# A planner that orders all instructions of a hybrid LRU, GLA and SSD backbone, with new prices for its instructions

## The chip, the core and the metric

The kernel runs on one core of one Trainium2 chip. A core has TensorE (PE in the profile, with its weight loads as PEld), VectorE (DVE), ScalarE (ACT), GpSimd (POOL) and a queue on SyncE (SP) that issues the DMAs. The engines run side by side, each through its own instructions in the order of the program, and wait for each other by semaphores. The metric is the device time of one execution in microseconds; the tables give the median of the runs.

## The reference

Two layers (`DEPTH` 2) over 512 latent tokens and 256 context tokens of width 1024. Each layer normalises and modulates the tokens, projects them once to 13408 columns, mixes them in three branches (an RG-LRU, a chunked gated linear attention GLA, and a Mamba-2 SSD, each in both directions), gates and projects each branch, merges them and projects the sum. Layer 1 returns only the latent tokens, so it needs the context only as far as its states go.

```python
for l in range(DEPTH):
    need_ctx = l < DEPTH - 1
    shift, scale, gate = jnp.split(jax.nn.silu(c) @ ada_w[l] + ada_b[l], 3, axis=-1)
    h_lat = _rmsnorm(x_lat, pre_g[l]) * (1.0 + scale[:, None]) + shift[:, None]
    h_ctx = _rmsnorm(x_ctx, pre_g[l]) * (1.0 + scale_c) + shift_c
    s_l = _split_cols(h_lat @ p['w_in'])          # and s_c of h_ctx
    # three branches, context first, their states handed to the latent scans
    y = LRU(s[0]), GLA(s[2], s[3], s[4], s[6]), SSD(s[8], s[9])
    pa = (ya * jax.nn.silu(s[1])) @ p['w_pa']
    pb = (_rmsnorm(yb, gla_norm_g) * jax.nn.silu(s[5])) @ p['w_pb']
    pc = _rmsnorm(yc * jax.nn.silu(s[7]), ssd_norm_g) @ p['w_pc']
    g = jax.nn.sigmoid(s[10])
    o = (g[0] * pa + g[1] * pb + g[2] * pc) @ p['w_out']
    x_lat = x_lat + gate[:, None] * _rmsnorm(o_lat, post_g[l])
```

## The kernel before

**The work.** All of it is float32. A large product is made of three passes of float32r matmuls: both operands are split into a high part (a cast) and a low part (the difference), and high x high, low x high and high x low are summed in PSUM. Weights come in items of 128 x 1024 numbers (512 KB): a DMA from SP loads one into one of two `raw` buffers; `splitter` cuts it into two halves and splits each into `wh` (a cast, by ACT or DVE, `copy`, L328 or L329) and `wl` (a subtraction on DVE, `sub`, L343), four buffers of each; `main` issues the matmuls of the items (`mm`, L388). One item of layer 0 is 24 pairs of matmuls with 256 and 512 columns; one of layer 1 that needs only the latent tokens is 24 with 512 columns. Results stand in two PSUM tiles `pp`, which an engine must empty before the next item but one can begin.

**The branches.** The SSD branch works in four groups: states (`ssd_update`: POOL makes `xw`, a copy and a subtraction split it into `xwh` and `xwl`, PE multiplies), masks (`ssd_ms`: a DMA broadcasts rows `cumd` into `rr`, ACT adds biases in eight steps of 128, DVE selects, ACT takes the exponential, POOL multiplies), outputs (`ssd_scan`: `y`, `yi`) and a group norm. GLA and LRU follow. In the LRU and merge part, `it_out` multiplies by `w_pa`; its tail needs a gate tile that an SP load brings back from DRAM (`load_gate`), and `gate_rows` sends a gain row to DRAM and back (`gpd`, `gp`). Then come the output projection and the residual (`it_wout`, `post`).

**What sets the order.** No order is written by hand. Every piece of work is a generator (a stream) that offers one instruction after another with a price in ns, and `loop` plans the whole program before it runs: it holds a modelled time for each engine and each tile, and of all instructions on offer it puts next the one that can start first by the model. `start_of` gives that start: the engine's free time, or the end of what writes or reads the tiles on another engine plus `LAT` (200 ns) and a slack by engine (1200 ns for PE, 100 for DVE and ACT, 0 for POOL and SP). Where an instruction can go to two engines (`any_op`: ACT or DVE for a copy, DVE or POOL for some subtractions), the one with the earlier modelled end gets it. Ties go to the stream with the higher rank. Each engine then runs its instructions in the order planned; the prices reach the chip in no other way.

```python
            for c in ins:
                if c.we != eng and c.w + slack > r:
                    r = c.w + slack
...
                    for w, (eng, cost, _) in enumerate(c[1]):
                        t = self.start_of(eng, c[2], c[3], LAT + SLACK[eng])
                        if w == 0 or t + cost < t0 + c0:
                            t0, c0, w0 = t, cost, w
                    k = (t0, 0 if s.urgent and s.urgent() else s.prio, s.seq)
                    if best is None or k < best[0]:
                        best = (k, s, w0)
```

The prices stand with the helpers: `any_op` (L206 to L211) for DMAs, whose modelled queue moves 360 bytes a ns and whose landing is put 2000 ns after that; `act` (L315), `copy` (L328) and `affine` (L335) for ACT; `sub` (L345), `tt` and `ts` for POOL; `vcost` for DVE; `mm` (L386) for PE.

Of the kernel before, what the change touches and what calls it, by code (L numbers as in the profile page):

```python
# [9 lines left out]
F32R = mybir.dt.float32r  # L10
I32 = mybir.dt.int32
AF = mybir.ActivationFunctionType
ALU = mybir.AluOpType
AX = mybir.AxisListType
PSUM = bass.MemoryType.PSUM
# [125 lines left out]
class Sched:  # L141
# [48 lines left out]
    def any_op(self, ways, outs, ins):  # L190

        outs = [self.cell(o) for o in outs]
        ins = [self.cell(i) for i in ins if i is not None and not isinstance(i, (int, float))]
        yield ("op", ways, outs, ins)
        eng, cost, emit = ways[self.way]
        start = self.start_of(eng, outs, ins)
        if eng == "PE":
            if start - self.eng_free[eng] > HAM_WINDOW:
                self.warm_up = HAM_WINDOW
            if self.warm_up > 0:  # L200
                cost *= 2
                self.warm_up -= cost
        extra = emit()
        if isinstance(extra, int):
            cost += extra
        if eng == "SP":  # L206
            self.eng_free[eng] = start + 470
            self.dma_free = max(start, self.dma_free) + cost
            fin = self.dma_free + 2000
        else:  # L210
            fin = self.eng_free[eng] = start + cost  # L211
        self.now = max(self.now, start)
        for c in outs:
            if fin > c.w:
                c.w, c.we = fin, eng
        for c in ins:
            if fin > c.r:
                c.r, c.re = fin, eng
# [56 lines left out]
class Mixer(Sched):  # L275
# [30 lines left out]
    def act(self, out, in_, func, bias=None, scale=None, accum=None):  # L306
        kw = {}
        if bias is not None:
            kw["bias"] = bias
        if scale is not None:  # L310
            kw["scale"] = scale
        if accum is not None:
            kw["accum_out"] = accum
        aps = sum(not isinstance(x, (int, float)) for x in (bias, scale) if x is not None)
        cost = 0.83 * out.free_size() + 60 + 90 * aps  # L315

        def emit():
            st = ACT_SETS.get(func)
            self.nc.scalar.activation(out, in_, func, **kw)  # L319
            if st and st != self.act_set:  # L320
                self.act_set = st
                return ACT_LOAD
        yield from self.op("ACT", [out] + ([accum] if accum is not None else []), [in_, bias, scale], cost, emit)

    def copy(self, out, in_):

        n = out.free_size()
        yield from self.any_op([("ACT", 0.83 * n + 60, lambda: self.nc.scalar.copy(out, in_)),  # L328
                                ("DVE", self.vcost(n, in_, True), lambda: self.nc.vector.tensor_copy(out, in_))],  # L329
                               [out], [in_])  # L330

    def affine(self, out, in_, scale, bias):

        n = out.free_size()
        yield from self.any_op([("ACT", 0.83 * n + 240, lambda: self.nc.scalar.activation(  # L335
                                    out, in_, AF.Identity, scale=scale, bias=bias)),
                                ("DVE", self.vcost(n, in_, True) + 120, lambda: self.nc.vector.tensor_scalar(
                                    out, in_, scale, bias, ALU.mult, ALU.add))], [out], [in_, scale, bias])

    def sub(self, out, a, b, pool=False):  # L340

        n = out.free_size()
        ways = [("DVE", self.vcost(n, a), lambda: self.nc.vector.tensor_tensor(out, a, b, ALU.subtract))]  # L343
        if pool:
            ways.append(("POOL", 2.3 * n + 50, lambda: self.nc.gpsimd.tensor_tensor(out, a, b, ALU.subtract)))  # L345
        yield from self.any_op(ways, [out], [a, b])

    def vcost(self, n, x, fast=False):
        return (0.52 if fast and x.space != PSUM else 1.04) * n + 69

    def tt(self, out, a, b, op, pool=False):
        eng = self.nc.gpsimd if pool else self.nc.vector
        cost = 2.3 * out.free_size() + 50 if pool else self.vcost(out.free_size(), a)
        yield from self.op("POOL" if pool else "DVE", [out], [a, b], cost, lambda: eng.tensor_tensor(out, a, b, op))  # L354

    def stt(self, out, a, s, b, op0, op1):
# [2 lines left out]

    def ts(self, out, a, s1, s2, op0, op1=None, pool=False):  # L360
        eng = self.nc.gpsimd if pool else self.nc.vector
        cost = 2.3 * out.free_size() + 50 if pool else \
            self.vcost(out.free_size(), a, True) + 60 * sum(not isinstance(s, float) for s in (s1, s2) if s is not None)

        def emit():
            if op1 is None:
                eng.tensor_scalar(out, a, s1, s2, op0)
            else:
                eng.tensor_scalar(out, a, s1, s2, op0, op1)
        yield from self.op("POOL" if pool else "DVE", [out], [a, s1, s2], cost, emit)  # L370
# [12 lines left out]

    def mm(self, out, lhsT, rhs, start, stop):
        n, m = rhs.free_size(), lhsT.free_size()
        cost = (max(n, 2 * m) if rhs.dtype == F32R else 4 * max(n, m)) / 2.4 + 1  # L386
        yield from self.op("PE", [out], [lhsT, rhs], cost,
                           lambda: self.nc.tensor.matmul(out, lhsT, rhs, start=start, stop=stop))  # L388

# [1574 lines left out]
```

## Time and profile before

| | us |
|---|---|
| median of 3 runs (2744.84 to 2748.49) | 2746.31 |
| the profiled execution | 2747.11 |
| its span, first to last instruction | 2745.4 |
| PE busy | 2681.3 (98%) |
| PEld busy | 2331.2 (85%) |
| DVE busy | 2075.3 (76%) |
| ACT busy | 1204.4 (44%) |
| POOL busy | 587.9 (21%) |

The profile is of one execution. A busy time is the time in which at least one instruction of that engine was under way, so an engine's idle time in a stretch is the stretch minus its busy time. Durations of neighbouring instructions of one engine can overlap; the spacing of their starts is what each adds. A line such as L388 is that of a helper, so the tiles' names (`wh`, `rr`, `xwl`) tell the pieces of work apart. Stretches are counted from the span's start. The granted TensorE clock was 0.997 of full speed over the span.

### The profile page before, as it was taken

How to read it: one execution, taken by the hardware profiler on the slowest of the kernel's cores; microseconds unless marked ns; L12 is line 12 of the kernel's file. 1: busy time of each engine (PE TensorE's matmuls, PEld its weight loads, DVE VectorE, ACT ScalarE, POOL GpSimd, SP SyncE). 2: the span in 40 equal slices, each digit the busy share in tenths (PEclk: the TensorE clock that was granted, in tenths of full speed). 3: DMA queues.
4: the chain of work that ended last, by engine and by line, in shares of the span. 5: the costliest groups of instructions: out<-in, count | busy, mean ns of one | idle time of the engine just before them, and what ended most of it. 6: DMA issues, size and time to landing. Idle time of an engine off the chain costs nothing.

```text
span 2745.4 us, 42859 instructions
## 1 busy us (share of the span) xinstructions
PE 2681.3 (98%) x16166; PEld 2331.2 (85%) x16166; DVE 2075.3 (76%) x3874; ACT 1204.4 (44%) x2312; POOL 587.9 (21%) x690
## 2 busy tenths in 40 slices
PE   7999999999999999999999999999999999999988
PEld 5888888888888888888889978787878888888878
DVE  5779888897555653568956888999898766568986
ACT  4356545454312332336712644545454333235743
POOL 1153525344000000001100224444352000001100
PEclk9999999999999999999999999999999999999999
DMA  6342423233352223452256433334343532243255
GB/s 212 83 123 74 112 66 112 74 100 86 106 182 74 74 62 92 151 175 61 71 169 208 154 93 104 95 89 105 81 111 112 169 85 77 83 148 103 58 157 198
DMA packets 448255, 307.99 MB, mean 112 GB/s; under 512 B 17188, under 2 KB 423280, under 8 KB 448048
## 3 DMA queue, kind: packets, MB, share of 16 engines
q1 hardware_dynamic: 448048, 305.26, 38.4%
q8 instruction: 127, 2.08, 0.3%
q14 instruction: 80, 0.66, 0.1%
HBM read 273.15 MB, written 32.06 MB: 111 GB/s over the span
## 4 chain that ended last, share of the span: by engine, by line
PE 75%; DVE 14%; DMA 4%; issue 3%; ACT 2%; POOL 2%; SPq 0%; DVEq 0%; POOLq 0%; ACTq 0%
PE pp L388 61%; PE aux L388 10%; DVE wl L343 2%; PE aux L392 2%; DMA rr<-cumd 2%; DVE r L358 1%; DMA ada<-in_ada_w_dram 1%; DVE wh L329 1%; DVE xa L358 1%; PE aux L524 1%; ACT rr L319 1%; DMA raw<-in_w_in_dram 1%; DVE xwl L343 0%; POOL ss L708 0%; DVE w L354 0%
## 5 line engine op out<-in xcount | busy, mean ns | idle before, releaser
L388 PE MATMUL pp<-hh,wh 128*128 128x256 f32 (+2 forms) x2624 | 759.8, 351 | 4.6 <-DVE xa L358 2.8
L388 PE MATMUL pp<-hl,wh 128*128 128x256 f32 (+2 forms) x2624 | 763.1, 352 | 0.1
L388 PE MATMUL pp<-hh,wl 128*128 128x256 f32 (+2 forms) x2624 | 760.5, 351 | 0.0
L388 PEld LDWEIGHTS pp<-hh,wh 128*128 128x128 f32 (+1 forms) x2624 | 485.2, 188 | 66.2 <-issue 1.9
L388 PEld LDWEIGHTS pp<-hl,wh 128*128 128x128 f32 (+1 forms) x2624 | 486.3, 188 | 60.1 <-issue 1.6
L388 PEld LDWEIGHTS pp<-hh,wl 128*128 128x128 f32 (+1 forms) x2624 | 486.6, 188 | 59.3 <-issue 1.9
L343 DVE TENSOR_TENSOR wl<-raw,wh 128x512 fp32r<-128x512 f32 (+1 forms) x628 | 477.7, 763 | 42.1 <-ACT wh L328 13.7
L329 DVE CAST wh<-raw 128x512 fp32r<-128x512 f32 (+1 forms) x372 | 181.4, 488 | 346.7 <-PE pp L388 334.6
L328 ACT CAST wh<-raw 128x512 fp32r<-128x512 f32 (+1 forms) x256 | 157.0, 618 | 305.4 <-PE pp L388 257.2
L319 ACT ACTIVATE rr<-rr,tokp 128x128 f32<-128x128 f32 x640 | 204.8, 391 | 120.0 <-DMA rr<-cumd 119.7
L319 ACT ACTIVATE r<-pp 128x768 f32<-128x768 f32 (+1 forms) x112 | 78.5, 701 | 220.8 <-PE pp L388 219.9
L354 POOL TENSOR_TENSOR xw<-xt,tokp 128x256 f32<-128x256 f32 x160 | 122.1, 763 | 238.8 <-ACT xt L328 66.0
L706 POOL TENSOR_SCALAR ss<-ss 128x1 f32<-128x1 f32 x52 | 17.7, 340 | 686.8 <-ACT ob L319 654.7
L354 POOL TENSOR_TENSOR rr<-rr,cb 128x512 f32<-128x512 f32 x80 | 112.7, 1409 | 147.6 <-ACT rr L319 139.9
L354 POOL TENSOR_TENSOR w<-av 128x768 f32<-128x768 f32 x32 | 51.7, 1617 | 420.9 <-ACT av L319 330.1
L388 PE MATMUL pp<-yh,wh 128*128 128x512 f32 (+1 forms) x384 | 117.2, 359 | 4.8 <-DVE r L358 4.2
L388 PE MATMUL pp<-ol,wh 128*128 128x512 f32 (+1 forms) x384 | 119.7, 365 | 0.0
L388 PE MATMUL pp<-oh,wh 128*128 128x512 f32 (+1 forms) x384 | 119.5, 361 | 0.0
L388 PE MATMUL pp<-oh,wl 128*128 128x512 f32 (+1 forms) x384 | 119.2, 361 | 0.0
L388 PE MATMUL pp<-yh,wl 128*128 128x512 f32 (+1 forms) x384 | 115.9, 356 | 1.7 <-DVE wl L343 1.7
L388 PE MATMUL pp<-yl,wh 128*128 128x512 f32 (+1 forms) x384 | 116.8, 358 | 0.2 <-DVE yl L358 0.2
L388 PE MATMUL pp<-wh,hh 128*128 128x256 f32 x384 | 109.1, 284 | 0.0
(267 smaller groups left out, 5308.3 us busy)
## 6 DMA issues: line engine op xcount, KB each, us to landing
raw<-in_w_in_dram SPq DMA_DIRECT2D x208, 512.0 KB, 4.1
rr<-cumd SPq DMA_DIRECT2D x160, 256.0 KB, 3.7
raw<-in_w_out_dram SPq DMA_DIRECT2D x40, 512.0 KB, 3.8
raw<-in_w_pc_dram SPq DMA_DIRECT2D x32, 512.0 KB, 3.7
raw<-in_ada_w_dram SPq DMA_DIRECT2D x32, 512.0 KB, 6.0
ada<-in_ada_w_dram SPq DMA_DIRECT2D x8, 1024.0 KB, 6.0
raw<-in_w_pb_dram SPq DMA_DIRECT2D x16, 512.0 KB, 4.1
raw<-in_w_pa_dram SPq DMA_DIRECT2D x16, 512.0 KB
```

What stands on the lines that cost most here:

```text
L319: self.nc.scalar.activation(out, in_, func, **kw)
L328: yield from self.any_op([("ACT", 0.83 * n + 60, lambda: self.nc.scalar.copy(out, in_)), ("DVE", self.vcost(n, in_, True), lambda: self.nc ...
L329: ("DVE", self.vcost(n, in_, True), lambda: self.nc.vector.tensor_copy(out, in_))],
L343: ways = [("DVE", self.vcost(n, a), lambda: self.nc.vector.tensor_tensor(out, a, b, ALU.subtract))]
L354: yield from self.op("POOL" if pool else "DVE", [out], [a, b], cost, lambda: eng.tensor_tensor(out, a, b, op))
L358: lambda: self.nc.vector.scalar_tensor_tensor(out, a, s, b, op0, op1))
L388: lambda: self.nc.tensor.matmul(out, lhsT, rhs, start=start, stop=stop))
L392: yield from self.op("PE", [out], [in_, idn], 108, lambda: self.nc.tensor.transpose(out, in_, idn))
L524: yield from self.op("PE", [ps], [self.scf, w], w.free_size() / 2.4, lambda: self.nc.tensor.matmul(out, lt, w, start=k < 4, stop=k >= 4, t ...
L706: yield from self.op("POOL", [r], [ss], 150, lambda: self.nc.gpsimd.tensor_scalar(r, ss, 1.0 / width, EPS, ALU.mult, ALU.add))
```

## The change

New prices in the planner, nothing else: the same streams, tiles, slots, ranks and slacks. A float32r matmul of n columns costs 0.4525 n ns where it cost n / 2.4 + 1, a float32 one 1.675 m + 2 where it cost 4 m / 2.4 + 1, m being the larger of its two widths. On ACT the fixed part of 60 ns becomes 72 for a source in PSUM and 100 for one in SBUF, with 92 more for an instruction that also accumulates. On POOL 2.3 n + 50 becomes 2.4 n + 100. A DMA lands 3000 ns after its modelled transfer, where it was 2000. DVE's prices, transposes and the condition matmuls stay.

```diff
--- before.py
+++ after.py
@@ -206,7 +206,7 @@
         if eng == "SP":
             self.eng_free[eng] = start + 470
             self.dma_free = max(start, self.dma_free) + cost
-            fin = self.dma_free + 2000
+            fin = self.dma_free + 3000
         else:
             fin = self.eng_free[eng] = start + cost
         self.now = max(self.now, start)
@@ -312,7 +312,7 @@
         if accum is not None:
             kw["accum_out"] = accum
         aps = sum(not isinstance(x, (int, float)) for x in (bias, scale) if x is not None)
-        cost = 0.83 * out.free_size() + 60 + 90 * aps
+        cost = self.acost(out.free_size(), in_) + 90 * aps + 92 * (accum is not None)
 
         def emit():
             st = ACT_SETS.get(func)
@@ -325,14 +325,14 @@
     def copy(self, out, in_):
 
         n = out.free_size()
-        yield from self.any_op([("ACT", 0.83 * n + 60, lambda: self.nc.scalar.copy(out, in_)),
+        yield from self.any_op([("ACT", self.acost(n, in_), lambda: self.nc.scalar.copy(out, in_)),
                                 ("DVE", self.vcost(n, in_, True), lambda: self.nc.vector.tensor_copy(out, in_))],
                                [out], [in_])
 
     def affine(self, out, in_, scale, bias):
 
         n = out.free_size()
-        yield from self.any_op([("ACT", 0.83 * n + 240, lambda: self.nc.scalar.activation(
+        yield from self.any_op([("ACT", self.acost(n, in_) + 180, lambda: self.nc.scalar.activation(
                                     out, in_, AF.Identity, scale=scale, bias=bias)),
                                 ("DVE", self.vcost(n, in_, True) + 120, lambda: self.nc.vector.tensor_scalar(
                                     out, in_, scale, bias, ALU.mult, ALU.add))], [out], [in_, scale, bias])
@@ -342,15 +342,21 @@
         n = out.free_size()
         ways = [("DVE", self.vcost(n, a), lambda: self.nc.vector.tensor_tensor(out, a, b, ALU.subtract))]
         if pool:
-            ways.append(("POOL", 2.3 * n + 50, lambda: self.nc.gpsimd.tensor_tensor(out, a, b, ALU.subtract)))
+            ways.append(("POOL", self.gcost(n), lambda: self.nc.gpsimd.tensor_tensor(out, a, b, ALU.subtract)))
         yield from self.any_op(ways, [out], [a, b])
+
+    def acost(self, n, x):
+        return 0.83 * n + (72 if x.space == PSUM else 100)
+
+    def gcost(self, n):
+        return 2.4 * n + 100
 
     def vcost(self, n, x, fast=False):
         return (0.52 if fast and x.space != PSUM else 1.04) * n + 69
 
     def tt(self, out, a, b, op, pool=False):
         eng = self.nc.gpsimd if pool else self.nc.vector
-        cost = 2.3 * out.free_size() + 50 if pool else self.vcost(out.free_size(), a)
+        cost = self.gcost(out.free_size()) if pool else self.vcost(out.free_size(), a)
         yield from self.op("POOL" if pool else "DVE", [out], [a, b], cost, lambda: eng.tensor_tensor(out, a, b, op))
 
     def stt(self, out, a, s, b, op0, op1):
@@ -359,7 +365,7 @@
 
     def ts(self, out, a, s1, s2, op0, op1=None, pool=False):
         eng = self.nc.gpsimd if pool else self.nc.vector
-        cost = 2.3 * out.free_size() + 50 if pool else \
+        cost = self.gcost(out.free_size()) if pool else \
             self.vcost(out.free_size(), a, True) + 60 * sum(not isinstance(s, float) for s in (s1, s2) if s is not None)
 
         def emit():
@@ -383,7 +389,7 @@
 
     def mm(self, out, lhsT, rhs, start, stop):
         n, m = rhs.free_size(), lhsT.free_size()
-        cost = (max(n, 2 * m) if rhs.dtype == F32R else 4 * max(n, m)) / 2.4 + 1
+        cost = max(0.4525 * n, 0.835 * m + 1) if rhs.dtype == F32R else 1.675 * max(n, m) + 2
         yield from self.op("PE", [out], [lhsT, rhs], cost,
                            lambda: self.nc.tensor.matmul(out, lhsT, rhs, start=start, stop=stop))
```

## Rows read from the trace of the kernel before

**Rows 1.** The page's head and part 1: span; busy us, share by engine

```profile
span 2745.4 us, 42859 instructions
PE 2681.3 (98%) x16166; PEld 2331.2 (85%) x16166; DVE 2075.3 (76%) x3874; ACT 1204.4 (44%) x2312; POOL 587.9 (21%) x690
```

**Rows 2.** Busy time by stretch: stretch, length, busy us by engine, clock, DMA share

```profile
0.00:45.00 45.00, 26.08 (x190) 12.98 (x191) 22.22 (x67) 19.77 (x40) 9.84 (x29) 0.95 0.88 281
45.00:1380.00 1335.00, 1330.69 (x8373) 1176.32 (x8372) 974.23 (x1830) 588.32 (x1127) 296.21 (x338) 1.00 0.35 98
1380.00:1600.00 220.00, 216.31 (x1467) 198.28 (x1466) 156.39 (x283) 83.17 (x174) 19.43 (x28) 1.00 0.55 177
1600.00:2050.00 450.00, 438.28 (x2393) 365.53 (x2394) 409.41 (x764) 230.66 (x516) 191.29 (x217) 1.00 0.35 94
2050.00:2420.00 370.00, 365.60 (x2135) 314.84 (x2134) 244.60 (x540) 119.33 (x213) 39.75 (x55) 1.00 0.37 106
2420.00:2655.00 235.00, 223.78 (x1091) 189.15 (x1090) 204.41 (x286) 134.28 (x183) 26.07 (x16) 1.00 0.37 111
2655.00:2746.00 91.00, 80.54 (x528) 74.10 (x526) 64.01 (x108) 28.83 (x62) 5.29 (x8) 0.95 0.59 195
```

**Rows 3.** Timeline of PE, its last matmul: start, us, engine, line, operation, tiles

```profile
2735.60 0.28 PE L388 MATMUL pp<-wh,ml 128*128 128x256 f32 x1
```

**Rows 4.** Chain that ended last, from 680 to 732 us: start, us, what

```profile
681.69 49.23 PE pp L388 x284
```

**Rows 5.** Groups of instructions on ACT and POOL: busy, mean ns, idle before

```profile
L328 ACT CAST wh<-raw 128x512 fp32r<-128x512 f32 (+1 forms) x256 | 157.0, 618 | 305.4 <-PE pp L388 257.2
L319 ACT ACTIVATE rr<-rr,tokp 128x128 f32<-128x128 f32 x640 | 204.8, 391 | 120.0 <-DMA rr<-cumd 119.7
L354 POOL TENSOR_TENSOR rr<-rr,cb 128x512 f32<-128x512 f32 x80 | 112.7, 1409 | 147.6 <-ACT rr L319 139.9
```

**Rows 6.** DMA issues: tiles, queue, count, KB each, median us to landing

```profile
raw<-in_w_in_dram SPq DMA_DIRECT2D x208, 512.0 KB, 4.1
rr<-cumd SPq DMA_DIRECT2D x160, 256.0 KB, 3.7
```

**Rows 7.** Waits of the whole span: who for whom, us, pieces, longest

```profile
DVE wh L329 <- PE pp L388: 334.6, 183, 7.0
ACT rr L319 <- DMA rr<-cumd: 119.7, 79, 4.6
```

**Rows 8.** Low half of a weight on DVE: group 2050 to 2420, timeline

```profile
L343 DVE TENSOR_TENSOR wl<-raw,wh 128x512 fp32r<-128x512 f32 x91 | 64.3, 709 | 8.9 <-ACT wh L328 2.4 <-PE pp L388 2.1
...
2640.90 1.29 DVE L343 TENSOR_TENSOR wl<-raw,wh 128x512 fp32r<-128x512 f32 x2
```

**Rows 9.** Groups of instructions on DVE from 1600 to 2050

```profile
L343 DVE TENSOR_TENSOR wl<-raw,wh 128x512 fp32r<-128x512 f32 x100 | 85.6, 857 | 5.2 <-ACT wh L328 1.5
L329 DVE CAST wh<-raw 128x512 fp32r<-128x512 f32 x50 | 31.7, 634 | 6.7 <-PE pp L388 6.6
```

**Rows 10.** Tile wh from 1600 to 2050: busy us of PE, PEld, DVE, ACT

```profile
1600.00:2050.00 450.00, 301.10 (x1078) 189.08 (x1079) 117.14 (x150) 30.23 (x49) 1.00 0.35 94
```

**Rows 11.** PE's waits from 1600 to 2050

```profile
PE aux L392 <- DVE r L358: 3.4, 5, 1.2
PE aux L388 <- DVE xwh L329: 2.4, 4, 1.0
```

**Rows 12.** PE's waits from 2420 to 2655

```profile
PE pp L388 <- DVE r L358: 4.2, 1, 4.2
PE pp L388 <- DVE xa L358: 3.2, 4, 1.4
```

**Rows 13.** Timeline around 2650 without PE: start, us, engine, what, idle before

```profile
2648.36 0.33 SPq L396 DMA_DIRECT2D gp<-gpd  x1
2648.74 0.42 SPq L396 DMA_DIRECT2D r<-g__3034_16505  x1
...
2653.86 0.69 DVE L358 SCALAR_TENSOR_TENSOR r<-r,pp 128x512 f32<-128x512 f32 x1 [5.55 <-DMA r<-g__3034_16505]
```

## The prediction

> **What bounds the kernel now.** The page comes first, then a table by stretch, because the share of busy time hides where an engine is short. TensorE is busy for 2681.3 of 2745.4 us [rows 1], and no other engine comes near it over the whole span. The change issues the same matmuls, transposes and loads, so TensorE's work stays and only its 64.1 us of idle time is at stake. The stage table [rows 2] places that idle time as stretch minus PE's busy time: 18.9 us in the first 45 us (the condition vectors and the first normalised tokens, with the DMA engines 88% busy); 4.3 us in the 1335 us of layer 0's mixer; 3.7 us from 1380 to 1600 (output projection of layer 0 and start of layer 1); 11.7 us from 1600 to 2050 (layer 1's SSD branch); 4.4 us in layer 1's GLA; 11.2 us in its LRU and merge; 10.5 us at the end, of which 9.5 stand behind the last matmul, which starts at 2735.60 [rows 3]. What to see: layer 0 is filled almost without a hole, and what an order can win lies in layer 1, in about 31 us between 1380 and 2655.
>
> A busy PE could still hide a slow pace, so the pace is read too. In 49.23 us PE runs 284 matmuls of 256 and 512 columns in turn without a break, 173.3 ns each [rows 4]. That is what the new price says: (0.4525 x 256 + 0.4525 x 512)/2 = 173.8; the old one said (107.7 + 214.3)/2 = 161.0. So PE runs at the pace of its matmuls there, which an order doesn't alter.
>
> **The change part by part.** Nothing is added to or removed from the work, and the costs touch the chip only through choices: which ready instruction the planner puts next, and whether a copy goes to ACT or DVE, a subtraction to DVE or POOL.
>
> Matmul prices: for 512 columns 214.3 becomes 231.7 ns, up 8.1%; the row bears out the new one. ACT: a 512-wide copy out of SBUF goes from 485 to 525 (up 8.2%); the trace's cast of that kind takes 618 and a 128-wide bias step, priced 256 and now 296, takes 391 [rows 5]. These durations overlap the next instruction, so they bound the true spacing from above; the new price is nearer. POOL: 512 wide, 1228 becomes 1329 (up 8.2%), and the row has 1409 [rows 5]. DMA: the 256 KB row broadcast is priced 728 + 2000 and now 728 + 3000 = 3.73 us, and lands in 3.7; the 512 KB weight load 3.46 and now 4.46, and lands in 4.1 [rows 6].
>
> So PE, ACT and POOL all get dearer by about the same 8%. Against each other they hardly move. Three things do move: DVE's prices stay, so DVE becomes 8% cheaper in comparison; the planner's fixed distances (200 ns, and 1200 ns more for PE) stay, so fewer matmuls fit into one; and a landing is put 1 us later.
>
> The later landing. ACT waits 119.7 us in 79 pieces for the row broadcast [rows 7], on average 1.5 us, with casts and evictions queued behind it on ACT. Put 1 us later, up to 79 us of ACT's waiting can go, as later instructions slip in front. But ACT is busy for 230.7 of 450 us in layer 1's SSD [rows 2], and the PE waits there name DVE outputs [rows 11]. I price it at -2 us, between 0 and -4. Its other edge: queue SP keeps issue order, so a store thought to land later can put other loads ahead of the one that waits for it. The largest single wait of layer 1, 4.2 us [rows 12], is of that kind: a gate load leaves SP at 2648.74, straight behind the gain row's load at 2648.36, and DVE gets it at 2653.86 [rows 13]. With the gain load placed later, the gate load may go first and most of the 4.2 us with it; if both slip, it grows by up to 1 us.
>
> The dearer matmul. DVE waits 334.6 us in 183 pieces for PE to give back a weight buffer [rows 7], with other work queued behind the waiting cast. Priced 8% faster than they run, the 24 matmuls that hold such a buffer seem to end too early, and the cast stands too far forward in DVE's order. Right prices move it back. Where DVE has time this costs PE nothing today (layer 0: 4.3 us of idle). In layer 1's LRU, DVE is busy 204.4 of 235 us [rows 2] and PE's waits are for its outputs [rows 12].
>
> The cheaper DVE, in comparison. In layer 1's GLA, with POOL at 11%, the subtraction of a weight half takes 709 ns and two of them in a row 1.29 us, so about 0.60 us each by spacing [rows 8]: the price of 601 holds. From 1600 to 2050, with POOL at 43%, the same instruction takes 857 and the cast, priced 335, takes 634 [rows 9]. So in the SSD branch DVE is underpriced, and the change leaves that while it corrects the other three. The choice of engine for a 512-wide copy had DVE ahead by 150 ns and now by 190, so some casts go from ACT to DVE. It has 49 weight casts on ACT in that stretch [rows 10]; a tenth is 5 x 0.634 = 3 us more for DVE, covered by its 40.6 us of idle time; a third is 10.4 us. Price for PE: +1 to +3 where it lands badly, 0 where covered, 10.4 at worst. The Trainium skill (SBUF — State Buffer, section "SBUF: two separate sides") says that DVE instructions with two SBUF inputs and GpSimd ones take a shared port pair by an exclusive lock, the later one waiting for all of the other's instruction. The trace agrees in direction (709 against 857 ns). By that rule no fixed price per DVE instruction can be right beside a busy POOL, and the slower rival below is what it would do.
>
> The sum against the profiled execution's own 2747.11 us (span 2745.4, 1.7 around it): start 0 (DMA-paced, -1 to +1); layer 0 +1 (a new order can hardly fill 4.3 us better, and could reopen as much: 0 to +4); 1380 to 1600 -0.5 (-1 to +1); layer 1's SSD 0, from -2 for the landing and +2 for DVE (-5 to +10); its GLA -0.5 (-2 to +1); LRU and merge -3 (-7 to +3); end 0, since the last steps have one order. Together -3.0, which is 2744.1; the median of the runs shown lies 0.8 below the profiled execution, so 2743 us.
>
> **The rivals.** *Faster*: the right prices close most of the holes they cause. For it: the holes of layer 1 lie behind late DVE outputs and one late load, not behind a full PE. Price: LRU and merge from 11.2 to 4 us, SSD from 11.7 to 7, the two others from 8.1 to 6, together -14: 2732 us. Against it: the PE waits are many and small (the largest group of the SSD stretch is 3.4 us in 5 pieces [rows 11]), and a new order makes new ones.
>
> *Slower*: DVE is overloaded in layer 1's SSD. A third of the 49 ACT casts goes over, 16 x 0.634 = 10.4 us, and all of it falls into runs in which PE already waits for DVE: 2747.1 + 10.4 - 0.8 = 2757 us. It decides once DVE's busy time there passes about 430 of 450 us (it has 409.4); below that its own idle time takes the surplus. For it: the PE waits there, 17 pieces in five groups of which [rows 11] shows the two largest, are all for DVE outputs. Against it: a difference of 40 ns in a choice that mostly hangs on queues microseconds long.
>
> *No effect in substance*: three engines scale alike, so most choices come out as before: 2746 us.
>
> **How the numbers follow.** The measurement can tell about 0.2%, or 5.5 us, from no change. My forecast, small gains against small losses, ends within that: 0.37. The rival without effect, 0.05, ends there too. Faster has 0.34, slower 0.24. So 0.34 faster, 0.42 within, 0.24 slower. The forecast's own range is 2741 to 2752. Adding all lower ends gives -16 and 2730; all upper ends +20 and 2766, which hardly meet, and I take 2759 above, so that about one case in ten stays out on each side.
>
> **What would show it.** Right: PE's busy time within 10 us of 2681; ACT's wait for the row broadcast well under 119.7 us; the wait of DVE's weight casts for PE shorter in the mean; the 4.2 us wait behind the gate load gone or under 2 us; PE idle in layer 0 between 4 and 8 us. DVE's casts up by 5 to 40 over the kernel, ACT's down by as many. Wrong: PE idle in layer 1's SSD over 18 us with DVE over 430, which is the slower rival; PE idle between 1380 and 2655 under 20 us, which is the faster one; or a longer start, where the 18.9 us hang on transfers that I took as fixed.

## The result, and the profile after

| | before | after |
|---|---|---|
| median, us | 2747.40 (2744.84 to 2748.54, 4 runs) | 2779.51 (2778.04 to 2781.45, 4 runs) |
| after / before | | 1.0119 (95%: 1.0101 to 1.0136) |
| span of the profiled execution, us | 2745.4 | 2778.3 |
| PE busy / idle, us | 2681.3 / 64.1 | 2701.1 / 77.2 |
| granted clock over the span | 0.997 | 0.992 |

The kernel is 32 us slower, 1.2%. The forecast of 2743 us and its range, 2730 to 2759, are both missed.

The page's head and part 1 of the kernel after, which answer to [rows 1] (span; then busy us, share of the span and number of instructions by engine):

```profile
span 2778.3 us, 42828 instructions
PE 2701.1 (97%) x16166; PEld 2344.8 (84%) x16166; DVE 2099.5 (76%) x3920; ACT 1186.7 (43%) x2274; POOL 584.2 (21%) x684
```

The same 16166 matmuls take PE 19.8 us more of busy time, and it is idle 13.1 us more. Together that is the 32.9 us of the span. Where: the table of busy time by stretch, cut after as many matmuls, to within a few, as [rows 2] (stretch, length, then busy us and instructions of PE, PEld, DVE, ACT and POOL, granted clock, DMA share, GB/s):

```profile
0.00:44.30 44.30, 26.25 (x191) 12.76 (x192) 21.45 (x68) 21.70 (x44) 10.41 (x29) 0.96 0.93 292
44.30:1394.80 1350.50, 1338.93 (x8376) 1178.72 (x8375) 994.40 (x1863) 577.74 (x1101) 295.17 (x331) 1.00 0.35 97
1394.80:1627.50 232.70, 224.04 (x1468) 202.87 (x1466) 159.63 (x284) 83.60 (x171) 20.53 (x28) 0.97 0.51 164
1627.50:2077.40 449.90, 437.95 (x2396) 367.89 (x2394) 407.38 (x771) 228.13 (x511) 198.92 (x225) 1.00 0.35 95
2077.40:2450.90 373.50, 367.72 (x2138) 316.66 (x2138) 245.02 (x538) 116.56 (x212) 27.14 (x47) 1.00 0.37 104
2450.90:2685.80 234.90, 226.87 (x1093) 193.23 (x1092) 203.72 (x282) 135.52 (x185) 26.71 (x16) 0.98 0.38 109
```

Set against before, with the boundaries of before moved so that both kernels have issued the same number of PE instructions at each, to within one (PE idle is length minus busy; the two kernels order them differently, so it is not always the same instruction):

| stretch | before: us / PE idle | after: us / PE idle | longer by | forecast |
|---|---|---|---|---|
| layer 0's mixer | 1335.3 / 4.3 | 1350.5 / 11.6 | +15.2 | +1 (0 to +4) |
| output projection, start of layer 1 | 220.2 / 3.7 | 232.7 / 8.7 | +12.5 | -0.5 (-1 to +1) |
| layer 1's SSD | 450.6 / 11.7 | 449.9 / 11.9 | -0.7 | 0 (-5 to +10) |
| layer 1's GLA | 370.1 / 4.4 | 373.5 / 5.8 | +3.4 | -0.5 (-2 to +1) |
| layer 1's LRU and merge | 237.4 / 11.2 | 234.9 / 8.0 | -2.5 | -3 (-7 to +3) |
| last products before the end | 76.8 / 0.3 | 82.7 / 3.7 | +5.9 | 0 |

Most of the loss stands where the forecast had seen little or nothing at stake, and the stretch it had feared for, layer 1's SSD, is unchanged. What PE waits for (engine, line and tile, released by what; us in total, times, longest us):

```profile
PE aux L530 <- DMA ada<-in_ada_w_dram: 10.0, 5, 4.1
PE pp L394 <- DVE wl L343: 5.8, 7, 2.1
PE pp L394 <- DVE xa L364: 5.6, 2, 3.5
PE aux L394 <- DVE xwh L329: 4.8, 8, 1.4
PE aux L394 <- DVE xwl L343: 4.5, 10, 0.9
PE aux L394 <- DVE xh L329: 4.3, 4, 1.7
PE aux L398 <- DVE ct L360: 4.0, 2, 2.7
```

Apart from the first line, which is the start, the lines shown are all outputs of DVE. Added over all groups of this view, PE waits 44.4 us for DVE where it waited 30.6 before; for DMAs 12.8 (14.4), for ACT 8.3 (7.1), for POOL 0.8 (0). So the waits for DVE grew by 13.8 us, about the whole of the 13.1 us of new idle time.

**One such wait, followed.** Timeline of the kernel after around the longest one, PE first, then DVE and POOL (start us, us, engine, line, operation, tiles, count, and in brackets the idle time before it and its releaser):

```profile
2609.41 0.39 PE L394 MATMUL pp<-hh,wl 128*128 128x512 f32 x1
2613.34 0.98 PE L394 MATMUL pp<-hh,wh 128*128 128x256 f32 x2 [3.54 <-DVE xa L364]
2614.11 0.84 PE L394 MATMUL pp<-hl,wh 128*128 128x256 f32 x2
...
2603.45 1.75 DVE L384 TENSOR_TENSOR_SCAN hf<-av,w 128x768 f32<-128x768 f32 x1
2605.12 0.66 DVE L384 TENSOR_TENSOR_SCAN hb<-av,w 128x256 f32<-128x256 f32 x1
2605.82 1.28 DVE L384 TENSOR_TENSOR_SCAN hb<-av,hb,w 128x512 f32<-128x512 f32 x1
2607.14 0.69 DVE L360 TENSOR_TENSOR hf<-hf,hb 128x512 f32<-128x512 f32 x1
2607.75 0.69 DVE L343 TENSOR_TENSOR wl<-raw,wh 128x512 fp32r<-128x512 f32 x1
2608.35 1.96 DVE L360 TENSOR_TENSOR hf<-hf,g 128x512 f32<-128x512 f32 x1
2610.23 2.96 DVE L364 SCALAR_TENSOR_TENSOR xa<-pp,p,xa 128x448 f32<-128x448 f32 x6
...
2607.85 1.91 POOL L360 TENSOR_TENSOR w<-av 128x768 f32<-128x768 f32 x1 [13.61 <-DVE hf L360]
```

DVE isn't idle: it runs without a gap, but the six `xa` steps, which empty the PSUM tile that PE's next item needs, stand in its queue behind three scans, two products and a weight subtraction. PE's next item stands in its own queue as if they were done by then, and PE stops for 3.54 us; 1.3 us of it come from the second product, which takes 1.96 us where the first takes 0.69. The pair of matmuls that starts at 2613.34 then takes 0.77 us to the next pair, where such a pair takes 0.35 elsewhere in this stretch: the clock has fallen.

**The clock.** Table by stretch of the kernel after, at the stretches with half the granted clock, 1.2 of 2.4 GHz (three of the seven between the start and the end, then the sum over all seven, then one beside the third; columns as above):

```profile
1567.60:1574.20 6.60, 5.67 (x26) 5.67 (x27) 4.39 (x9) 1.46 (x5) 0.43 (x2) 0.50 0.35 83
1618.80:1625.40 6.60, 5.98 (x22) 4.63 (x22) 5.01 (x10) 2.13 (x4) 0.00 (x0) 0.50 0.31 79
2611.90:2618.80 6.90, 5.46 (x18) 5.02 (x19) 6.66 (x11) 3.06 (x5) 1.47 (x1) 0.51 0.11 25
...
sum 37.10, PE 33.72 PEld 29.46 DVE 26.45 ACT 10.05 POOL 5.82; mean PE 4.82 PEld 4.21 DVE 3.78 ACT 1.44 POOL 0.83
...
2618.80:2625.70 6.90, 6.90 (x41) 6.14 (x41) 6.80 (x10) 5.11 (x5) 0.00 (x0) 1.00 0.31 76
```

In 6.9 us PE gets through 41 matmuls at the full clock, and through 18 at half of it (with 5.46 of the 6.90 us busy). In the seven such stretches of the kernel after, 37.1 us, PE is busy for 33.7; at half the pace about 16.9 us of that are lost, by this estimate. In the kernel before there is one, 3.4 us just behind its 4.2 us wait for the gate load [rows 12], so 1.7 us lost:

```profile
2654.90:2658.30 3.40, 3.40 (x9) 2.63 (x9) 2.79 (x5) 1.15 (x1) 0.00 (x0) 0.50 0.72 198
```

The difference, 15 us, is the larger part of the 19.8 us by which PE's busy time grew; the other 5 us were not traced.

The other groups that the forecast rests on, after the change, answering to [rows 5, 7] (groups: busy us, mean ns, idle before; then two waits):

```profile
L329 DVE CAST wh<-raw 128x512 fp32r<-128x512 f32 (+1 forms) x401 | 191.7, 478 | 369.1 <-PE pp L394 362.8 <-DMA raw<-in_w_in_dram 2.3 <-DMA raw<-in_w_pc_dram 1.3
L328 ACT CAST wh<-raw 128x512 fp32r<-128x512 f32 (+1 forms) x227 | 138.7, 617 | 241.3 <-PE pp L394 203.5 <-DMA raw<-in_w_in_dram 19.9 <-ACT mh L319 6.0
```
```profile
DVE wh L329 <- PE pp L394: 362.8, 186, 7.0
ACT rr L319 <- DMA rr<-cumd: 108.2, 69, 5.2
```

29 weight casts went from ACT (256) to DVE (372 before).

### The profile page after: what moved, and what is told of

Read it like the earlier page. It is cut to its first block, busy times and chain, and to the rows that moved or that the text cites. A ratio compares the mean times of both kernels' runs of the same rounds, so it can differ in the third digit from the quotient of the medians.

```text
span 2778.3 us, 42828 instructions
## 1 busy us (share of the span) xinstructions
PE 2701.1 (97%) x16166; PEld 2344.8 (84%) x16166; DVE 2099.5 (76%) x3920; ACT 1186.7 (43%) x2274; POOL 584.2 (21%) x684
## 4 chain that ended last, share of the span: by engine, by line
PE 74%; DVE 18%; issue 3%; DMA 2%; ACT 2%; POOL 1%; SPq 0%; DVEq 0%; POOLq 0%; ACTq 0%
PE pp L394 61%; PE aux L394 10%; DVE wl L343 2%; PE aux L398 2%; DVE r L364 2%; DVE xa L364 1%; DVE wh L329 1%; DMA ada<-in_ada_w_dram 1%; DVE xwl L343 1%; DVE rr L388 1%; DMA rr<-cumd 1%; PE aux L530 1%; DVE y L360 1%; DVE hf L360 0%; DVE xwh L329 0%
## 5 line engine op out<-in xcount | busy, mean ns | idle before, releaser
L343 DVE TENSOR_TENSOR wl<-raw,wh 128x512 fp32r<-128x512 f32 (+1 forms) x628 | 467.8, 748 | 44.6 <-ACT wh L328 15.3
L329 DVE CAST wh<-raw 128x512 fp32r<-128x512 f32 (+1 forms) x401 | 191.7, 478 | 369.1 <-PE pp L394 362.8
L319 ACT ACTIVATE rr<-rr,tokp 128x128 f32<-128x128 f32 x640 | 202.5, 390 | 108.6 <-DMA rr<-cumd 108.2
L328 ACT CAST wh<-raw 128x512 fp32r<-128x512 f32 (+1 forms) x227 | 138.7, 617 | 241.3 <-PE pp L394 203.5
L394 PE MATMUL pp<-wh,hl 128*128 128x256 f32 x384 | 108.9, 284 | 0.0
```

What stands on the lines that cost most here:

```text
L328: yield from self.any_op([("ACT", self.acost(n, in_), lambda: self.nc.scalar.copy(out, in_)), ("DVE", self.vcost(n, in_, True), lambda: se ...
```

## The experiments

Three theories were set against each other.

- **Ratio** (R; the first expectations call it theory A): the planner's order is good or bad by how dear DVE's work is in comparison to PE's. Correcting PE and leaving DVE made DVE look 8% quicker than it had looked, and consumers on PE are put where DVE isn't done.
- **Slack** (L): the fixed distances (200 ns, 1200 ns more for PE) now span fewer matmuls, so there is less margin before PE.
- **Scatter** (B): any change of the prices shakes the order into another one, and times scatter by 1% or so. The first two are its opposite, a cause that has a direction.

Where no interval is given, a time is one run, beside the kernel before on the same chip. The kernel before itself lay between 2737.9 and 2748.5 in all runs shown here, so a single time holds to some 5 us.

### Scatter: prices changed by next to nothing

Before, with `LAT` 201 instead of 200, and before, with each matmul 0.1 ns dearer; after, with `LAT` 201:

```diff
-LAT = 200
+LAT = 201
```
```diff
-        cost = (max(n, 2 * m) if rhs.dtype == F32R else 4 * max(n, m)) / 2.4 + 1
+        cost = (max(n, 2 * m) if rhs.dtype == F32R else 4 * max(n, m)) / 2.4 + 1.1
```

> The kernel before with the planner's fixed distance at 201 ns instead of 200: no price is better or worse for it, only near ties fall the other way. Theory A (the new prices are worse in kind: DVE too cheap beside the others): 2747 us, within 6. Theory B (scatter: the order before is a lucky draw, and any other order costs the holes that the clock gate then widens): 2755 to 2790 us, with more half-speed stretches of TensorE's clock than the one that the order before has between 47 and 2740 us.

> The kernel before with every matmul 0.1 ns dearer (under 0.1%). Theory A: 2747 us, within 6. Theory B: 2755 to 2790 us, and at other places than in the run with 201 ns.

> The changed kernel with the planner's fixed distance at 201 ns, to see whether its 2780 us are one unlucky order. If the loss is systematic (theory R): 2765 to 2790 us. If it is the scatter of near ties: as likely under 2760 as over.

Measured: 2743.57 and 2738.65 us, with 2743.87 before; and 2781.46, with 2744.65 before. Neighbours of before stay within some 5 us of it, a neighbour of after stays with after. Theory A had 2747 within 6 us for the first two, so the second lies 2 us outside; neither comes near the 2755 or more of theory B, and the third lies where theory R put it. Scatter of this size exists, but 32 us is not scatter. The two neighbours also show how far single rows of a trace move with next to no cause: weight casts on DVE 369 and 383 (before: 372), PE's waits for DVE 27.2 and 25.0 us (30.6), ACT's wait for the row broadcast 108.8 and 93.1 us (119.7).

### Which price: the change's parts alone

Only the matmul prices of the change on the kernel before; only the landing; only ACT's prices. The price of POOL was not tried alone.

```diff
-        cost = (max(n, 2 * m) if rhs.dtype == F32R else 4 * max(n, m)) / 2.4 + 1
+        cost = max(0.4525 * n, 0.835 * m + 1) if rhs.dtype == F32R else 1.675 * max(n, m) + 2
```
```diff
-            fin = self.dma_free + 2000
+            fin = self.dma_free + 3000
```
```diff
-        cost = 0.83 * out.free_size() + 60 + 90 * aps
+        cost = self.acost(out.free_size(), in_) + 90 * aps + 92 * (accum is not None)
... copy and affine likewise
```

> The kernel before with the new matmul prices alone. Theory A: the dear matmul makes DVE, ACT and POOL all look cheap, so this part carries most of the loss: 2765 to 2785 us, with layer 0's SSD losing first, as in the changed kernel (+9 us by 345 us from the start). Theory B: anywhere from 2745 to 2785, with no tie to where the changed kernel lost.

> The kernel before with the later DMA landing alone (3000 ns). By the prediction 2744 us: ACT's wait for the row broadcast falls from 119.7 us to under 60. Theory A: 2740 to 2750, since this price was wrong and is right now. Theory B: 2745 to 2785 all the same, although the wait falls.

> The kernel before with the new ACT prices alone, so ACT is dearer and all else stands. Theory R puts the loss on PE's price against DVE's and none here: 2738 to 2752 us. By the rival that the higher ACT price drives copies to DVE and overloads it: 2752 to 2765, with DVE's weight casts up from 372 by 20 or more.

Measured: matmul prices alone 2786.94 (2743.87 before), landing alone 2745.61 (2743.87), ACT's prices alone 2756.32 (2744.65). So the right matmul prices cost 43 us, more than the whole change; the landing does nothing that could be seen; ACT's prices cost about 12. The first is 2 us above the range of theory A; the second is within it, though ACT's wait for the broadcast stays at 95.0 us, not under 60; the third falls outside the range of theory R and into that of its rival, whose sign, 20 more weight casts on DVE, did not come (382). PE's waits with the matmul prices alone, behind the start's line (columns as above):

```profile
PE pp L388 <- DVE xa L358: 9.4, 5, 2.5
PE aux L388 <- DVE xwh L329: 7.2, 16, 1.7
PE aux L392 <- DVE r L358: 6.9, 9, 1.4
```

Outputs of DVE head the list as after the change; PE waits 50.6 us for DVE in all. The other direction for ACT, after with ACT's prices of before:

```diff
-        cost = self.acost(out.free_size(), in_) + 90 * aps + 92 * (accum is not None)
+        cost = self.acost(out.free_size(), in_) + 90 * aps
...
-        return 0.83 * n + (72 if x.space == PSUM else 100)
+        return 0.83 * n + 60
```

> The changed kernel with ACT's old prices. If ACT's price adds its 11 us to the loss: 2762 to 2772 us. If the matmul price alone makes all of it, as the run with that price alone (2787 us) suggests: 2775 to 2790.

Measured: 2768.52 (2744.10 before), 11 us under the kernel after, or 8 if each is set against before on its own chip. ACT's part is much the same from both sides. Why it costs was not followed further: alone it moved ten weight casts to DVE (382), no more than a neighbour of before has (383), and PE's wait for ACT rose from 7.1 to 13.0 us while that for DVE fell to 25.4.

### Ratio against slack

The ratio restored in the kernel after, by making DVE's prices 8.2% dearer, too; all else as changed:

```diff
-        return (0.52 if fast and x.space != PSUM else 1.04) * n + 69
+        return 1.082 * ((0.52 if fast and x.space != PSUM else 1.04) * n + 69)
```

> The changed kernel with DVE's prices up by 8.2% as well, so that PE, ACT, POOL and DVE stand to each other as before. Theory R (the ratio of DVE's price to PE's decides): 2740 to 2755 us, most of the 33 us come back, and PE's idle time falls from 77 to under 68 us. Theory L (the planner's fixed distance of 1400 ns from a result to its matmul now spans fewer matmuls): still 2770 to 2790, since that distance is as short as in the changed kernel.

> The changed kernel with DVE's prices up by 8.2%, in rounds: 0.993 to 0.996 of the time before by theory R, as in the one look (2731 us beside 2746). If that was the luck of one execution: 0.997 to 1.001.

The ratio of after, made in the kernel before by a cheaper DVE, PE and slack untouched; and the ratio moved the other way in before, by cheaper matmuls:

```diff
-        return (0.52 if fast and x.space != PSUM else 1.04) * n + 69
+        return ((0.52 if fast and x.space != PSUM else 1.04) * n + 69) / 1.0814
```
```diff
-        cost = (max(n, 2 * m) if rhs.dtype == F32R else 4 * max(n, m)) / 2.4 + 1
+        cost = (max(n, 2 * m) if rhs.dtype == F32R else 4 * max(n, m)) / 2.6 + 1
```

> The kernel before with DVE's prices down by 8.1% and all others, matmuls too, as they were: the ratio of the run with the new matmul price alone (2787 us), but the fixed distance as before. Theory R: 2775 to 2795 us. Theory L: 2740 to 2752.

> The kernel before with matmuls priced 8% lower still (2.6 columns a ns). Theory R, if it holds on this side too: the same as before or a little better, 2735 to 2748 us. Theory L says the same sign, 2735 to 2745, as the distance then spans more matmuls. A price that were best where it is right would make this 2755 or more.

And the slack raised in the kernel after:

```diff
-SLACK = {"PE": 1200, "DVE": 100, "ACT": 100, "POOL": 0, "SP": 0}
+SLACK = {"PE": 1500, "DVE": 100, "ACT": 100, "POOL": 0, "SP": 0}
```

> The changed kernel with PE's slack at 1500 ns instead of 1200 (a matmul is placed 1700 ns after its operand's end, where it was 1400). Theory L: 2745 to 2755 us, and fewer PE waits for xwh, xwl and r. Theory R: the ratio is untouched, so 2770 to 2785.

Measured: with the ratio restored 2730.71 in one run and 2731.94 in five (2730.97 to 2733.72), 0.9957 of before (0.9943 to 0.9971); before with a cheaper DVE 2776.14; before with cheaper matmuls 2737.99; after with more slack 2753.26.

The first is nearly 48 us below the kernel after, by one factor on DVE's prices (44 if each is set against before on its own chip). It also has the fixed distances that the slack theory blames, and that theory's 2770 to 2790 is missed. The second takes the slack theory's cause away, leaves only DVE's price against the others, and is as slow as the kernel after: its layer 0 is 18.1 us longer than before's, its next stretch 8.5; the slack theory had 2740 to 2752. With the matmul prices alone, which leave DVE, ACT and POOL as they stood to each other, the loss is there too. So the ratio of DVE's price to PE's is what brings the loss and what takes it away.

More slack mends 26 us without touching the ratio. There the slack theory had the right range and theory R, with 2770 to 2785, the wrong one: a larger distance serves as a margin against DVE's lateness. The number of casts stays 401 on DVE and 227 on ACT, PE's wait for DVE falls to 36.7 us, its idle time from 77.2 to 69.0, and its busy time from 2701.1 to 2682.5, with 6.8 us at half the granted clock between start and end instead of 37.1.

The ratio doesn't explain all. The kernel with the ratio restored is 12 us faster than the kernel before, which has the same ratio. Which of the prices in which the two differ does that was not tried.

The kernel with the ratio restored: its page's part 1, what PE waits for, and the DVE queue at the same matmul that waited 3.54 us above (there it starts at 2566.76 and waits for nothing):

```profile
PE 2680.2 (98%) x16166; PEld 2334.1 (85%) x16166; DVE 2079.7 (76%) x3856; ACT 1214.0 (44%) x2329; POOL 595.0 (22%) x691
```
```profile
PE aux L530 <- DMA ada<-in_ada_w_dram: 9.4, 4, 4.2
PE aux L394 <- DVE xh L329: 3.7, 4, 2.1
PE aux L398 <- DMA r<-in_c_ctx_dram: 2.7, 1, 2.7
PE aux L394 <- ACT th L319: 2.5, 1, 2.5
```
```profile
2562.07 0.96 DVE L360 TENSOR_TENSOR w<-w,th 128x768 f32<-128x768 f32 x1 [0.77 <-ACT w L319]
2562.96 2.97 DVE L364 SCALAR_TENSOR_TENSOR xa<-pp,p,xa 128x448 f32<-128x448 f32 x6
2565.84 0.95 DVE L360 TENSOR_TENSOR w<-w,th 128x768 f32<-128x768 f32 x1
2566.71 1.75 DVE L384 TENSOR_TENSOR_SCAN hf<-av,w 128x768 f32<-128x768 f32 x1
...
2566.76 0.51 PE L394 MATMUL pp<-hh,wh 128*128 128x256 f32 x2
```

The `xa` steps now stand ahead of the scan, DVE has a pause before them, and they end at 2565.93, before PE wants the tile. The waits for `xa`, `wl`, `xwh` and `xwl` have left the head of the list; PE's idle time is 50 us.

### How far: the price of DVE against a right price of PE

```diff
-        return (0.52 if fast and x.space != PSUM else 1.04) * n + 69
+        return 1.18 * ((0.52 if fast and x.space != PSUM else 1.04) * n + 69)
```

and the same with 1.25.

> The changed kernel with DVE's prices up by 18%, which is what the spacing of DVE instructions that follow each other without a gap is above its price in the trace of before (1.17 to 1.19 times, in the mean). Theory R, in its full form (all prices right in the mean): 2722 to 2735 us, at or below the 2731 of the run with 8.2%. If only the old ratio mattered and not the right one: 2735 to 2760, worse than with 8.2%. Theory L: 2770 or more.

> The changed kernel with DVE's prices up by 25%, now above the mean spacing of the trace. Theory R with an optimum at the right ratio: 2730 to 2750, past the best. Theory R with a margin that only has to be large enough: 2720 to 2735, as with 18%.

Measured: 1.18 gives 2737.02 (2734.17 to 2741.19, ten runs), 0.9974 of before (0.9965 to 0.9984); 1.25 gives 2752.91 in one run (2744.65 before). Theory R in its full form wanted 2735 or less at 1.18, no worse than at 1.082, and missed; 1.25 lies above both ranges, past the best. The kernels by DVE's price over that of a float32r matmul, 1.00 being that of after (for before, 231.7 / 214.3 = 1.08), with PE's waits added over all groups of the view:

| DVE to PE | kernel | us | PE waits for DVE / ACT / POOL, us |
|---|---|---|---|
| 1.00 | matmul prices alone | 2786.9 | 50.6 / 7.4 / 1.0 |
| 1.00 | after | 2779.5 | 44.4 / 8.3 / 0.8 |
| 1.00 | before, DVE cheaper | 2776.1 | 40.6 / 6.2 / 0.5 |
| 1.08 | before | 2747.4 | 30.6 / 7.1 / 0 |
| 1.08 | after, DVE x 1.082 | 2731.9 | 19.4 / 7.4 / 0.5 |
| 1.17 | before, matmuls cheaper | 2738.0 | 20.9 / 9.9 / 0.5 |
| 1.18 | after, DVE x 1.18 | 2737.0 | 17.7 / 15.6 / 3.9 |
| 1.25 | after, DVE x 1.25 | 2752.9 | 25.6 / 17.9 / 2.8 |

Too cheap, and PE waits for DVE; too dear, and work goes to ACT and POOL until PE waits for these. What heads the waits at 1.18, behind the start's 9.4:

```profile
PE pp L394 <- ACT yh L319: 6.4, 1, 6.4
PE pp L394 <- DVE wl L343: 4.4, 4, 1.4
PE aux L394 <- POOL xwl L345: 3.9, 6, 2.1
```

The bottom is broad, from 1.08 to 1.18. Which value in it is best stays open: neighbours scatter by 5 us, as much as the kernels with the right price of PE differ at 1.08 and 1.18. Nor do PE's waits order all the kernels: with ACT's prices alone they are 25.4 and 13.0 us for DVE and ACT, in sum about before's, and the time is 2756.3.

### The two uses of a price: which instruction next, or which engine

After, with a DVE dearer by 8.2% only where an engine is chosen; and the kernel with the ratio restored, with the engine chosen by DVE's plain price:

```diff
+                        cc = cost * 1.082 if eng == "DVE" else cost
-                        if w == 0 or t + cost < t0 + c0:
-                            t0, c0, w0 = t, cost, w
+                        if w == 0 or t + cc < t0 + c0:
+                            t0, c0, w0 = t, cc, w
```
```diff
+                        cc = cost / 1.082 if eng == "DVE" else cost
... and vcost times 1.082, as above
```

> The changed kernel, in which only the choice between two engines sees DVE's price raised by 8.2%; the modelled times stay those of the changed kernel. If the loss comes from casts that go to DVE: 2735 to 2755 us, with DVE's busy time back from 2099 to about 2080. If it comes from the order: 2768 to 2785.

> The changed kernel with DVE's modelled times raised by 8.2%, while the choice between two engines sees the plain price. If the order carries the loss: 2730 to 2750 us although the casts stay on DVE as in the changed kernel (about 400). If the casts carry it: 2768 to 2785.

Measured: 2769.10 and 2734.15 (2744.10 before). Of the 48 us between the kernel after and the one with the ratio restored, the price in the choice alone gives 10, the modelled durations alone 45 (7 and 42 of 44, if each is set against before on its own chip). The weight casts of the second:

```profile
L330 DVE CAST wh<-raw 128x512 fp32r<-128x512 f32 (+1 forms) x360 | 175.1, 486 | 350.0 <-PE pp L395 344.3 <-DMA raw<-in_w_in_dram 2.7 <-DMA raw<-in_w_pb_dram 0.8
L329 ACT CAST wh<-raw 128x512 fp32r<-128x512 f32 (+1 forms) x268 | 164.1, 618 | 330.5 <-PE pp L395 279.4 <-DMA raw<-in_w_in_dram 22.9 <-ACT sq L320 9.1
```

The two uses were not kept apart as meant. The price in the choice moved few casts back (401 to 392 on DVE, whose busy time stays at 2099.9 us), and with the longer modelled durations the casts on DVE fell to 360, not the 400 or so expected and close to the 354 of the kernel with the ratio restored: a DVE that the model holds busy for longer is chosen less, whatever price the choice sees. That casts alone don't make the loss shows elsewhere: with 401 of them on DVE the kernel with more slack takes 2753.3 us, and a neighbour of before with 383 takes 2738.7. So most of the loss comes in through the modelled durations, by when the model believes that DVE is done. How much of it is the order of the instructions and how much their engine was not separated.

## Why the prediction was wrong, step by step

**"Only its 64.1 us of idle time is at stake", busy time "within 10 us of 2681".** This step failed by 19.8 us. The forecast took PE's pace from an undisturbed stretch [rows 4] and PE's busy time as fixed. It had the row that speaks against it within reach: 3.4 us of half clock stand behind the gate load's wait of [rows 12]. After the change each of the waits of PE over 2 us (2.05, 2.09, 2.69 and 3.54 us) has a stretch of half clock beside it, so a hole can cost more than its length.

**"DVE becomes 8% cheaper in comparison."** The observation was right, and its sign too: it was put down as a loss. The step that failed is its size and place: the sum put +2 for it into layer 1's SSD. It was priced by the casts that change engine alone, at +1 to +3 and 10.4 at worst, in layer 1's SSD alone. The runs show 10 us for the price in the choice of engine, over the whole kernel and not in that stretch, and 45 us for the modelled durations, which had no term in the sum at all. A relative price moves every DVE instruction in the plan; I followed only those that can go to another engine. Behind it stands the premise that prices nearer to the trace give a better order: the right matmul prices alone cost 43 us. The term for layer 0, at most +4 because "DVE has time", was 15.2; the term for 1380 to 1600, at most +1, was 12.5. In layer 0 DVE is busy for 974.2 of 1335 us before [rows 2], and that mean share didn't tell whether it is done when a consumer is due.

**"The price of 601 holds."** It rested on one pair of subtractions [rows 8]. It holds for an instruction that stands alone: over the trace of before, the median spacing of weight subtractions that follow the instruction ahead without a gap is 609 ns. The mean is 761 in the SSD stretches of both layers and 682 elsewhere. Over all DVE instructions that stand in such rows, summed spacing over summed price is 1.19 in the SSD stretches (1622 instructions) and 1.17 elsewhere (1323). So DVE had been 17 to 19% underpriced all along, PE 8%, and correcting PE alone made the pair worse. The broad bottom from 1.08 to 1.18 fits that; that the two have the same reason was not shown, and the kernel with all DVE prices at 1.18 is no faster than that with 1.082.

**The slower rival** had the right sign and the wrong mechanism: layer 1's SSD is no longer than before, DVE is busy there for 407.4 of 449.9 us, not over 430, and PE idle for 11.9, not over 18.

**The later landing** was to be worth -2. Alone it gives 2745.61 against 2743.87, nothing that could be told. ACT's wait for the row broadcast is 95.0 us in 66 pieces alone and 108.2 in 69 with the whole change, not well below 119.7 as said, and within what neighbours of before have with the old landing price (108.8 and 93.1); no group of PE's waits for ACT names it.

**The dearer matmul** was to shorten DVE's wait for a weight buffer. Its mean went from 1.83 us (334.6 / 183) to 1.95 (362.8 / 186), which is within what the neighbours of before have (1.95 with `LAT` 201, 1.74 with the 0.1 ns). With the right matmul prices alone it is 2.06 (360.8 / 175), with matmuls priced lower still 1.66 (315.7 / 190): no run shows the dearer matmul to shorten it, and these two point the other way.

**What held, and what of it was luck.** The 4.2 us wait behind the gate load is gone; 24 matmuls later PE waits 1.3 us for another output of DVE. LRU and merge is 2.5 us shorter, of the 3 forecast, but the 1.3 us stand just behind its end, and with the stretch that follows it is 3.4 us longer. The gate load did go ahead of the gain row's load, as forecast, but not for the reason given. With the later landing alone (first two lines: start, us, queue, line, tiles) it still stands behind it, and PE still waits 4.2 us; with the matmul prices alone, at the old landing (last two lines), it goes first:

```profile
2647.15 0.33 SPq L396 DMA_DIRECT2D gp<-gpd  x1
2647.53 0.43 SPq L396 DMA_DIRECT2D r<-g__3034_16505  x1
...
2684.93 0.70 SPq L396 DMA_DIRECT2D r<-g__3034_16505  x1
2692.64 0.33 SPq L396 DMA_DIRECT2D gp<-gpd  x1
```

DVE's casts rose by 29, ACT's fell by as many, as forecast. The start did not move (18.0 us of idle time, 18.9 before), nor did the steps behind the last matmul. The faster rival's 2732 us is what the kernel with the ratio restored reaches, by a price that the change didn't have, with holes closed between 1380 and 2655 as that rival said (15.9 us of idle time there, 34.4 after the change, 31.0 before).

## What to carry to other kernels

Where a planner orders work by prices, their ratios can count before their values: correcting three engines of four to what a trace shows made this kernel 1.2% slower, and correcting the fourth by the same factor made it 0.4% faster than it had been. Judge a price by the instruction's mean spacing in its real company, not by its undisturbed duration alone (that pricing DVE at that mean is best was not shown: 2737.0 us, against 2731.9 with the smaller factor), and keep a margin in front of the engine that bounds the kernel: 300 ns more of it gave back 26 of 32 us here. And when costing a new order for an engine that is 98% busy, follow the producers of its operands, not its idle time alone, and look at what the granted clock is beside its present waits.

## What the runs showed of the hardware

**A wait can cost clock, too, but not each one does.** In the kernel after, waits of 1.75 us (at 1298) and 1.77 us (at 2442) left PE at 2.4 GHz, one of 1.40 (at 1771) was beside 3.4 us at 1.2 GHz. Longer ones are no surer: in the kernel with the ratio restored, waits of 2.05 us (at 1331) and 2.5 us (at 2585) each have 3.4 us of half clock beside them in one execution and none in another. Nor does the time at half clock order the kernels: that with cheaper matmuls has 27.2 us of it between start and end and takes 2738.0, before has 3.4 and takes 2747.4. So it makes a loss larger, and doesn't by itself decide which kernel is slower.

**DVE beside POOL.** In the timeline above the product `hf<-hf,g` at 2608.35 takes 1.96 us where the one ahead of it, of the same width, takes 0.69; POOL's product runs from 2607.85 to 2609.76. Over the trace of before, 478 weight subtractions of 512 with no POOL instruction of over 0.6 us beside them take 688 ns in the mean, and hardly vary (nine in ten lie between 678 and 694); the 146 that overlap one take 1016 in the mean, up to 2.3 us. By the Trainium skill (SBUF — State Buffer, section "SBUF: two separate sides") DVE instructions with two SBUF inputs and GpSimd ones share a port pair by an exclusive lock, the later one waiting for the whole of the other's instruction; these rows agree. That would account for the spread of the subtractions in the SSD stretches; the 17% in stretches where POOL does little stay open.
